# A 31-tap depthwise convolution as three of half length, with the tap tables, the LayerNorm mean and the block order changed beside it

## The chip, the cores and the metric

The kernel runs on one core of a Trainium2 chip. The metric is the device time of one execution in microseconds; the time shown is the median of three runs. A core has five engines with instruction streams of their own: TensorE (PE; its weight loads are listed as PEld), VectorE (DVE), ScalarE (ACT), GpSimd (POOL) and SyncE (SP), which issues all DMAs of this kernel.

## What is computed

One layer of a hybrid encoder block, f32, 1024 positions, width 1024. The part that matters here is the mixer with the long convolution, which runs beside a gated delta rule over 8 heads:

```python
h = rms_norm(x, g_mix); proj = h @ w_in      # columns: glu_a glu_b q k v z a_in b_in gate_a gate_b
c = glu_a * sigmoid(glu_b)
c = depthwise_conv(c, conv_dw_w) + conv_dw_b                 # 31 taps, centred, per channel
c = silu(layer_norm(c, conv_ln_g, conv_ln_b)); y_conv = c @ w_conv_out
q, k, v = split(silu(depthwise_conv(qkv, qkv_conv_w)))       # 5 taps
o = delta_rule(q, k, v) + reverse(delta_rule(reversed))      # then rms_norm * silu(z)
y = sigmoid(gate_a) * y_conv + sigmoid(gate_b) * (o @ w_delta_out)
x = x + y @ w_o                              # then a SwiGLU feed-forward, an embedding, a last RMSNorm
```

## The kernel before, in words

**Layout.** Activations lie transposed: 128 channels on partitions, positions along the free axis. A block column is 128 output channels of one projection: `block_half` makes 24 products of 128x128 by 512 for each half of the positions (8 slices of the contraction, three products each, since an f32 operand is split into a high and a low f32r part, `split`, L693). So a block column is 48 products.

**An order written out by a planner.** The program does not issue instructions directly. Each call (`pn.matmul`, `pn.act`, `pn.stt`, ...) adds an operation with an engine, a cost and a rank (`pn.level`); `Plan.order` (L346) then lays them out as a list scheduler: on each engine the ready operation with the lowest rank goes first, then the earlier one in the program. Each engine's order is fixed by that before the kernel runs; DMAs are issued on SP in planned order too. The ranks are in `LV` (L572): weights -3.0, delta rule -1.8, z 0.5, GLU 1.2, q/k/v 1.3, LayerNorm 2.1, gates 2.3, output projection of the convolution (cout) 2.4, and last the 31-tap convolution, 2.7. Tiles are planned as well: a request waits until its pool has a free buffer and its kind is under its cap (`CAP`, L573). The pool of large tiles (128 x 1024 f32) has `N_BIG` = 32 buffers: 16 hold the normed input as high and low parts, 1 the sum for the LayerNorm (`lnacc`), at most `N_D` = 11 belong to the delta rule; the rest is for block columns in flight.

**The stages.** Start: x is loaded, transposed and normed; tap tables are built (L825 to L838: 24 transposes of 5 taps into `cw5`, 8 of 31 taps into `cw31`). Then the block columns of `MAIN` and `FILL` (L597) in that program order: q, k, v (`do_qkv`, L912: projection, 5 taps on VectorE, SiLU, store), g (`do_glu`, L929), z and the gates a and b; `conv_out` (L1293); and the delta rule, four groups of two heads, whose chain steps are short f32 products with VectorE and ScalarE between them. By rank the delta rule goes first wherever it is ready and block columns fill in. The first block column's weights are loaded ahead (`first_w`, L792), at a fixed place, that of k0.

**The 31 taps.** `do_glu` writes the gated product into a tile padded by 15 positions on each side and calls `conv` (L896): the first tap on ScalarE with the bias, then 30 multiply-adds on VectorE, each over 1024 positions, each onto the one before (`scalar_tensor_tensor`). The result is stored to DRAM and added to `lnacc`.

**The LayerNorm.** `conv_out` waits for all eight blocks: it sums `lnacc` over channels by 8 products with one column of ones (`sums`, L753), scales, spreads the mean over partitions by 8 products with the identity (`rows`, L746), and for each half of the positions reads the blocks back, subtracts, squares and sums, then normalises, applies SiLU and projects by `w_conv_out` (cout: 8 x 24 products per half).

**After it.** The delta output projection (from L1398), with `OT_AFTER` and `WO_AFTER` tying its loads to stores of cout; then `w_o`, with `YT_AFTER` (which store its input's loads wait for) and `WO_LEAD` (how many output blocks start on the first half of the contraction before the second), the feed-forward, the embedding and the output.

L243 and L248 are the helpers of products and transposes, L268 and L275 those of ScalarE, L291 that of VectorE: in the profile all work has these lines, and the tiles tell it apart.

## Time and profile before

| | us |
|---|---|
| median of 3 runs (2107.71 to 2111.0) | 2109.98 |
| the profiled execution | 2112.86 |
| its span, first to last instruction | 2111.1 |
| busy: PE, PEld, DVE, ACT, POOL | 2071.5, 1701.3, 1639.3, 1143.8, 129.1 |

Busy time counts a matmul from its start to its modelled end, so a TensorE that is slowed down between products can look busy. The idle time of an engine that isn't the bottleneck costs nothing. DMA engines move 139 GB/s on the mean.

### The profile page before, as it was taken

The numbers are of one execution on the slowest core, as the hardware profiler recorded it, in microseconds if no ns is written. First come the engines' busy times: TensorE is split into PE (matmuls) and PEld (weight loads), VectorE is DVE, ScalarE is ACT, GpSimd is POOL, SyncE is SP. The second block draws the span as 40 slices with busy tenths as digits, with TensorE's granted clock in tenths as the row PEclk, the third lists the DMA queues.
The fourth block names the chain that finished last, engine by engine and source line by source line (L and its number), as shares of the span: only waits on it lengthen the run. The fifth ranks groups of instructions, "written<-read, shape, count | busy, mean of one in ns | idle before, by whom it ended". The sixth has DMA issues, their size and how long they took to land.

```text
span 2111.1 us, 29502 instructions
## 1 busy us (share of the span) xinstructions
PE 2071.5 (98%) x10279; PEld 1701.3 (81%) x10279; DVE 1639.3 (78%) x2683; ACT 1143.8 (54%) x2603; POOL 129.1 (6%) x197
## 2 busy tenths in 40 slices
PE   8999999999999999999999999999999999999998
PEld 6888888788888788878877788887777777777888
DVE  5578969877999899996687767787666657888776
ACT  6726674657766664857875444433333335443542
POOL 1000111011200211001100000000000000000000
PEclk9999999999999999999999999999999999999999
DMA  6334332533333421544567686433333337442253
GB/s 220 126 102 134 106 118 68 179 95 111 135 101 115 140 83 68 199 149 161 165 206 234 204 278 209 127 120 105 100 96 104 100 99 264 154 160 80 66 161 104
DMA packets 296726, 292.85 MB, mean 139 GB/s; under 512 B 17945, under 2 KB 217810, under 8 KB 296576
## 3 DMA queue, kind: packets, MB, share of 16 engines
q1 hardware_dynamic: 296576, 290.95, 42.8%
q8 instruction: 81, 1.33, 0.3%
q14 instruction: 69, 0.57, 0.1%
HBM read 205.10 MB, written 85.79 MB: 138 GB/s over the span
## 4 chain that ended last, share of the span: by engine, by line
PE 64%; DVE 6%; ACT 4%; issue 1%; DMA 1%; POOL 0%; DVEq 0%; SPq 0%; POOLq 0%; ACTq 0%
PE ps L243 63%; DVE big L291 4%; ACT big L268 2%; PE ps L248 1%; DVE mid L291 1%; DVE w L291 1%; ACT big L275 1%; ACT w L268 0%; ACT m L275 0%; DMA raw<-in_w_delta_out_dram 0%; ACT mid L268 0%; POOL rn L320 0%; DMA mid<-d 0%; DMA big<-dqkv 0%; DMA big<-dg 0%
## 5 line engine op out<-in xcount | busy, mean ns | idle before, releaser
L243 PE MATMUL ps<-big,w 128*128 128x512 f32 (+1 forms) x7416 | 1825.7, 400 | 5.7 <-ACT w L268 3.9
L243 PEld LDWEIGHTS ps<-big,w 128*128 128x128 f32 x7416 | 1360.2, 189 | 316.6 <-ACT w L268 5.8
L291 DVE SCALAR_TENSOR_TENSOR big<-big,cw 128x1024 f32<-128x1024 f32 x336 | 433.5, 1295 | 17.3 <-ACT big L275 11.2
L268 ACT CAST w<-raw 128x512 fp32r<-128x512 f32 (+2 forms) x308 | 185.5, 607 | 275.0 <-PE ps L243 225.8
L291 DVE TENSOR_TENSOR w<-raw,w 128x512 fp32r<-128x512 f32 (+2 forms) x308 | 208.9, 681 | 85.9 <-ACT w L268 83.1
L268 ACT CAST w<-mid 128x512 fp32r<-128x512 f32 (+1 forms) x185 | 108.3, 588 | 153.6 <-PE ps L243 121.9
L291 DVE TENSOR_TENSOR big<-big 128x512 fp32r<-128x512 f32 (+2 forms) x238 | 161.5, 702 | 12.0 <-ACT big L268 8.4
L291 DVE TENSOR_TENSOR w<-mid,w 128x512 fp32r<-128x512 f32 (+1 forms) x185 | 118.7, 644 | 60.3 <-ACT w L268 59.4
L291 DVE TENSOR_TENSOR big<-ps,big 128x512 f32<-128x512 f32 (+1 forms) x146 | 99.9, 687 | 36.6 <-PE ps L243 27.2
L268 ACT CAST big<-big 128x512 fp32r<-128x512 f32 x163 | 96.2, 622 | 43.7 <-DVE big L291 23.3
L268 ACT COPY big<-big 32x128 f32<-32x128 f32 (+1 forms) x264 | 103.1, 441 | 18.7 <-DVE big L291 16.8
L243 PE MATMUL ps<-big 128*128 128x128 f32 (+1 forms) x784 | 104.6, 280 | 7.8 <-ACT big L268 5.1
L243 PEld LDWEIGHTS ps<-big 128*128 128x128 f32 x784 | 98.9, 191 | 16.4 <-issue 11.2
L268 ACT COPY big<-ps 128x512 f32<-128x512 f32 (+3 forms) x178 | 74.9, 429 | 65.3 <-PE ps L243 56.2
L275 ACT ACTIVATE mid<-mid 128x512 f32<-128x512 f32 (+2 forms) x87 | 50.4, 584 | 51.9 <-DVE mid L291 28.4
L243 PEld LDWEIGHTS ps<-S,big 128*128 128x128 f32 x448 | 69.2, 190 | 11.4 <-DVE S L291 2.9
L243 PE MATMUL ps<-S,big 128*128 128x128 f32 x448 | 74.9, 276 | 0.6 <-DVE S L291 0.6
L268 ACT COPY m<-ps 128x512 f32<-128x512 f32 x52 | 30.4, 587 | 76.8 <-PE ps L243 76.7
L268 ACT COPY mid<-ps 128x512 f32<-128x512 f32 x71 | 41.1, 585 | 55.5 <-PE ps L243 45.7
L248 PE MATMUL ps<-ident,big 128*128 128x128 f32 (+2 forms) x368 | 61.1, 280 | 9.9 <-DMA big<-in_x_dram 4.9
L243 PEld LDWEIGHTS ps<-big,m 128*128 128x128 f32 x512 | 62.6, 194 | 7.6 <-ACT m L275 5.3
L275 ACT ACTIVATE big<-big 128x1024 f32<-128x1024 f32 (+2 forms) x80 | 56.7, 718 | 22.0 <-DVE big L291 18.6
(161 smaller groups left out, 1717.6 us busy)
## 6 DMA issues: line engine op xcount, KB each, us to landing
raw<-in_w_in_dram SPq DMA_DIRECT2D x128, 256.0 KB, 3.1
mid<-d SPq DMA_DIRECT2D x120, 256.0 KB, 3.6
d<-big SPq DMA_DIRECT2D x119, 256.0 KB, 3.0
big<-d SPq DMA_DIRECT2D x119, 256.0 KB, 5.1
d<-mid SPq DMA_DIRECT2D x100, 256.0 KB, 2.1
big<-dqkv SPq DMA_DIRECT2D x32, 512.0 KB, 5.1
raw<-in_w_gate_up_dram SPq DMA_DIRECT2D x50, 256.0 KB, 3.1
dqkv<-big SPq DMA_DIRECT2D x24, 512.0 KB, 2.6
```

Source lines behind the costliest of these rows:

```text
L243: o = self.add("pe", lambda: self.nc.tensor.matmul(out.ap(), lhsT.ap(), rhs.ap(), start=start, stop=stop, **kw), [out], [lhsT, rhs], cost)
L248: self.add("pe", lambda: self.nc.tensor.transpose(out.ap(), in_.ap(), ident.ap()), [out], [in_, ident], 0.11)
L268: return self.nc.scalar.copy(out.ap(), in_.ap())
L275: return self.nc.scalar.activation(out.ap(), in_.ap(), func, **kw)
L291: return getattr(e, name)(**{k: v.ap() if isinstance(v, View) else v for k, v in kw.items()})
```

## The change

The 31 taps are split into even and odd positions. With even taps w0, w2, ... (16) and odd taps w1, w3, ... (15), and the padded input kept as its odd places `co` and even places `ce`, three sums of half length give both results: u = (w_even + w_odd) on co; the even outputs are u plus the even taps on ce - co; the odd outputs are u plus the odd taps on (ce one place on) - co. So a block takes 15 + 16 + 15 multiply-adds over 512 elements and two subtractions over 527 and 526, instead of 30 over 1024; the first tap on ScalarE is 512 wide. The last multiply-adds of the two results write at stride two into the tile that held the padded input, which is the block's output from then on (`acc = c[:, :T]`). A tile `dif` holds the two differences.

The 5-tap and 31-tap rows are loaded into one tile and turned by 8 transposes of 46 rows into one table `taps`; sums of neighbouring taps are added up in `cw31s`. The LayerNorm's mean comes from one f32 product of the 128x128 ones with `lnacc` for each half, which gives it on all partitions at once. The first block's weights follow the order's first entry (now q0). Ranks, caps, the order of blocks, `YT_AFTER` and `WO_LEAD` have new values.

```diff
@@ -569,8 +569,8 @@
 
 
 N_BIG, N_MID, N_W, N_D = 32, 8, 6, 11
-LV = dict(w=-3.0, logits=-0.2, delta=-1.8, qkv=1.3, glu=1.2, z=0.5, conv31=2.7, gate=2.3, pl=-0.3, ln=2.1, cout=2.4)
-CAP = dict(raw5=6, acc5=3, cpad=10, acc31=1, lnev=3, wmain=4, wfill=2, bank=2, x0=4)
+LV = dict(w=-3.6, logits=-0.2, delta=-1.8, qkv=1.3, glu=1.5, z=0.5, conv31=3, gate=2.3, pl=-0.3, ln=0.9, cout=2.4)
+CAP = dict(raw5=6, acc5=3, cpad=10, acc31=1, dif=1, lnev=3, wmain=4, wfill=2, bank=2, x0=4)
 LEAD = (1, 3, 3)
 PAIRS = (3, 3, 3)
 NS = sum(PAIRS)
@@ -581,8 +581,8 @@
 WO_AFTER = 12
 RE_CAP = 3
 O_CAP = 4
-YT_AFTER = (2, 1)
-WO_LEAD = 6
+YT_AFTER = (1, 1)
+WO_LEAD = 5
 WO_BANKS = 6
 FIN = 3
 X_LEVEL = -4
@@ -594,9 +594,9 @@
 
 
 
-MAIN = ("k0 q0 v0 l0 g0 z0 k1 q1 z2 v1 g1 z1 q3 k2 g2 v3 v2 q2 k3 k4 q4 z3 z4 a4 k5 g3 v5 z6 v4 g4 "
-        "v6 q5 k7 q6 a5 g5 a7 k6 z5 z7 g6 v7 g7 a6 q7")
-FILL = "a0 a2 a3 a1 b0 b1 b2 b3 p0 b4 b5 b6 b7"
+MAIN = ("q0 k0 v0 l0 g0 z0 k1 q1 z2 v1 g1 g2 z1 k2 v3 v2 q3 z3 q2 k3 k4 a4 z4 q4 k5 g3 v5 z6 v4 g4 v6 q5 "
+        "k7 q6 g6 a5 g5 a7 k6 z5 v7 g7 a6 q7 z7")
+FILL = "a0 a2 b5 b7 a3 a1 b2 b0 b1 b3 p0 b4 b6"
 PL_AFTER = 2
 
 
@@ -686,8 +686,8 @@
     e_t = const("e_t", [P, 16, NJ])
     e_l = const("e_l", [P, 16, NJ])
     pl_r = const("pl_r", [P, NJ])
-    cw31 = const("cw31", [P, KB, CK])
-    cw5 = const("cw5", [P, 24, SK])
+    taps = const("taps", [P, KB, CK + 3 * SK])
+    cw31s = const("cw31s", [P, KB, CK // 2 + 1])
 
 
     def split(hi, lo, src, scale=None):
@@ -789,7 +789,8 @@
 
     n = vectors(0, VEC[:1])
     pn.stream = "main"
-    first_w = [load_w(w_in[0], 0, KB, C_Q + NH * P)]
+    first = MAIN.split()[0]
+    first_w = [load_w(w_in[0], 0, KB, C_Q + ("qkv".index(first[0]) * NH + int(first[1:])) * P)]
     pn.stream = "start"
     for t in range(4, 8):
         pn.dma(x0[t], x[0, t * P:(t + 1) * P, :])
@@ -822,20 +823,20 @@
 
     to(0.9, "tables")
     vectors(n, VEC[1:])
-    ps = bank()
+
+    NT = CK + 3 * SK
+    raw = large([NT, D], line="taps")
+    pn.dma(raw[:CK], conv_dw_w[0])
     for i in range(3):
-        c5 = large([SK, D], line="taps", cap=2)
-        pn.dma(c5, qkv_conv_w[0, :, i * D:(i + 1) * D])
-        for k in range(KB):
-            o = (i * KB + k) * SK
-            pn.transpose(ps[:, o:o + SK], c5[:, cs(k)], ident[:SK, :SK])
-    pn.copy(cw5, ps[:, :24 * SK].fold(24, SK))
-    c31 = large([CK, D], line="taps", cap=2)
-    pn.dma(c31, conv_dw_w[0])
+        pn.dma(raw[CK + i * SK:CK + (i + 1) * SK], qkv_conv_w[0, :, i * D:(i + 1) * D])
     ps = bank()
     for k in range(KB):
-        pn.transpose(ps[:, k * CK:(k + 1) * CK], c31[:, cs(k)], ident[:CK, :CK])
-    pn.copy(cw31, ps[:, :KB * CK].fold(KB, CK))
+        pn.transpose(ps[:, k * NT:(k + 1) * NT], raw[:, cs(k)], ident[:NT, :NT])
+    pn.copy(taps, ps[:, :KB * NT].fold(KB, NT))
+    cw31 = taps[:, :, :CK]
+
+    pn.tt(cw31s[:, :, :CK // 2], taps.at(0, [(NT, KB), (2, CK // 2)]), taps.at(1, [(NT, KB), (2, CK // 2)]), ALU.add)
+    pn.copy(cw31s[:, :, CK // 2:], cw31[:, :, CK - 1:])
 
 
     d_g = dp.tile([P, P], tag="dg", bufs=1)
@@ -920,11 +921,34 @@
         pn.fill(raw[:, 0:2], 0.0)
         pn.fill(raw[:, T + 2:T + 4], 0.0)
         acc = large(line="acc5", cap=CAP["acc5"])
-        conv(acc, raw, cw5[:, b], SK)
+        conv(acc, raw, taps[:, hd, CK + which * SK:CK + (which + 1) * SK], SK)
         pn.act(acc, acc, AF.Silu)
         pn.dma(d_qkv[which][hd], acc)
 
     lnacc = large(line="lnacc")
+    CH = (T + CK - 1) // 2
+
+    def conv31(c, b):
+
+
+
+        w, ws = cw31[:, b], cw31s[:, b]
+        co, ce = c[:, :CH], c[:, CH:2 * CH]
+        dif = large([P, 2, CH], line="dif", cap=CAP["dif"])
+        pn.tt(dif[:, 0], ce, co, ALU.subtract)
+        pn.tt(dif[:, 1, :CH - 1], ce[:, 1:], co[:, :CH - 1], ALU.subtract)
+        acc = large([P, 2, HW], line="acc31", cap=CAP["acc31"])
+        u, v = acc[:, 0], acc[:, 1]
+        pn.act(u, co[:, 0:HW], AF.Identity, scale=ws[:, 0:1], bias=col["cb31"][:, b:b + 1])
+        n = CK // 2
+        for t in range(1, n + 1):
+            pn.stt(u, co[:, t:t + HW], ws[:, t:t + 1], u, ALU.mult, ALU.add)
+        for t in range(n + 1):
+            pn.stt(c.at(0, [(2, HW)]) if t == n else v, dif[:, 0, t:t + HW], w[:, 2 * t:2 * t + 1],
+                   v if t else u, ALU.mult, ALU.add)
+        for t in range(n):
+            pn.stt(c.at(1, [(2, HW)]) if t == n - 1 else u, dif[:, 1, t:t + HW], w[:, 2 * t + 1:2 * t + 2],
+                   u, ALU.mult, ALU.add)
 
     def do_glu(b):
         to(LV["glu"], "main", "glu")
@@ -933,15 +957,18 @@
         for h in range(2):
             pn.act(sg[h], block_half(wb, hA, h, KB), AF.Sigmoid)
         wa = load_cols(C_GLUA + b * P)
+
         c = large([P, T + CK - 1], line="cpad", cap=CAP["cpad"])
         for h in range(2):
             pa = block_half(wa, hA, h, KB)
-            pn.tt(c[:, 15 + h * HW:15 + (h + 1) * HW], pa, sg[h], ALU.mult)
-        pn.fill(c[:, 0:15], 0.0)
-        pn.fill(c[:, T + 15:T + 30], 0.0)
+            pn.tt(c.at(7 + h * HW // 2, [(CH + 1, 2), (1, HW // 2)]), pa.at(0, [(1, 2), (2, HW // 2)]),
+                  sg[h].at(0, [(1, 2), (2, HW // 2)]), ALU.mult)
+        pn.fill(c[:, 0:7], 0.0)
+        pn.fill(c[:, CH - 8:CH + 8], 0.0)
+        pn.fill(c[:, 2 * CH - 7:2 * CH], 0.0)
         to(LV["conv31"], "conv31")
-        acc = large(line="acc31", cap=CAP["acc31"])
-        conv(acc, c, cw31[:, b], CK, bias=col["cb31"][:, b:b + 1])
+        conv31(c, b)
+        acc = c[:, :T]
         for h in range(2):
             pn.dma(d_y[b][h], acc[:, hs(h)])
         if b == 0:
@@ -1292,13 +1319,12 @@
 
     def conv_out():
         to(LV["ln"], "fill", "ln")
-        mean = tin.tile([P, NJ], tag="mean", bufs=1)
-        ps = sums(lnacc, NJ)
-        pn.ts(mean, ps[:, :NJ], 1.0 / D, ALU.mult)
         for h in range(2):
             to(LV["ln"], "fill", "ln")
             mb = mid.tile([P, HW], tag="lnb", line="lnb", bufs=3)
-            pn.act(mb, rows(mean[:, 4 * h:4 * h + 4], 4))
+            ps = bank()
+            pn.matmul(ps, ones, lnacc[:, hs(h)], True, True)
+            pn.act(mb, ps, AF.Copy, scale=1.0 / D)
             acc = mid.tile([P, HW], tag="lnb", line="lnb", bufs=3)
 
             def centred(k):
```

## Rows read from the trace of the kernel before

**Rows 1.** Part 1 of the page (busy time, share of the span, instructions of each engine) and, of part 2, the clock granted to TensorE in 40 slices of the span, in tenths of full speed.

```profile
PE 2071.5 (98%) x10279; PEld 1701.3 (81%) x10279; DVE 1639.3 (78%) x2683; ACT 1143.8 (54%) x2603; POOL 129.1 (6%) x197
...
PEclk9999999999999999999999999999999999999999
```

**Rows 2.** Busy time by stretch of the span: length, then busy us and number of instructions of each engine, the granted clock, the share of the DMA engines, GB/s.

```profile
0.00:50.00 50.00, 43.10 (x214) 32.07 (x215) 26.59 (x47) 34.99 (x66) 5.70 (x19) 0.94 0.67 229
...
150.00:950.00 800.00, 788.39 (x4239) 658.45 (x4238) 704.97 (x1133) 508.22 (x1365) 92.25 (x133) 1.00 0.37 120
950.00:1200.00 250.00, 238.72 (x1257) 198.74 (x1256) 185.71 (x330) 176.15 (x402) 19.69 (x24) 0.97 0.60 190
...
1500.00:1750.00 250.00, 250.00 (x1069) 198.65 (x1068) 150.05 (x227) 89.83 (x153) 0.00 (x0) 1.00 0.34 108
2100.00:2111.00 11.00, 1.58 (x13) 1.10 (x11) 4.27 (x11) 3.06 (x9) 1.08 (x2) 0.78 0.26 95
```

**Rows 3.** The same stretches for TensorE's instructions that read a weight tile w alone (apart from the 256-wide ones at the very end these are all products of 512 columns): length, busy us and number, clock, DMA share, GB/s.

```profile
0.00:50.00 50.00, 16.14 (x52) 0.94 0.67 229
...
150.00:950.00 800.00, 663.37 (x2527) 1.00 0.37 120
950.00:1200.00 250.00, 193.28 (x721) 0.97 0.60 190
...
1500.00:1750.00 250.00, 250.00 (x1069) 1.00 0.34 108
2100.00:2111.00 11.00, 0.00 (x0) 0.78 0.26 95
```

**Rows 4.** TensorE's order of time in the delta stage: start us, us, engine, line, operation, out<-in, shape, number of instructions merged.

```profile
1008.69 3.73 PE L243 MATMUL ps<-big,m 128*128 128x128 f32 x32
1012.17 1.41 PE L243 MATMUL ps<-big,w 128*128 128x512 f32 x5
```

**Rows 5.** What TensorE waited for from 150 to 950 us: us in total, number of waits, longest us.

```profile
PE ps L243 <- ACT big L268: 3.8, 3, 1.7
PE ps L243 <- DVE xin L291: 2.7, 4, 0.9
...
PE ps L248 <- DVE m L291: 1.4, 3, 0.7
```

**Rows 6.** TensorE's groups of instructions by shape over the whole span: out<-in, shape, xcount | busy us, mean ns of one | idle us before them. An f32 product is two instructions, an f32 transpose one.

```profile
L243 PE MATMUL ps<-ones,big 128*128 128x1 f32 x32 | 3.8, 244 | 0.0
...
L248 PE MATMUL ps<-ident,big 5*128 5x5 f32 x24 | 2.3, 203 | 0.0
L243 PE MATMUL ps<-ident,mean 128*128 128x128 f32 x16 | 2.3, 275 | 0.0
...
L248 PE MATMUL ps<-ident,big 31*128 31x31 f32 x8 | 1.0, 225 | 0.1
```

**Rows 7.** VectorE's groups by shape over the whole span: xcount | busy us, mean ns of one | idle us before them.

```profile
L291 DVE SCALAR_TENSOR_TENSOR big<-big,cw 128x1024 f32<-128x1024 f32 x336 | 433.5, 1295 | 17.3 <-ACT big L275 11.2
...
L291 DVE TENSOR_TENSOR big<-big 128x512 f32<-128x512 f32 x68 | 46.2, 687 | 2.9 <-DMA big<-d 1.7 <-DVE w L291 0.4 <-DMA d<-big 0.3
...
L291 DVE SCALAR_TENSOR_TENSOR mid<-ps,vec_t,mid 128x512 f32<-128x512 f32 x16 | 11.3, 745 | 0.4 <-PE ps L248 0.3
...
L291 DVE TENSOR_TENSOR mid<-mid 128x128 f32<-128x128 f32 x2 | 0.6, 292 | 0.1
...
L291 DVE TENSOR_TENSOR mid<-ps,bc 128x128 f32<-128x128 f32 x1 | 0.3, 292 | 3.1 <-ACT beta L275 3.1
```

**Rows 8.** VectorE's order of time where eleven taps of one block run one behind the other: start us, us, number merged.

```profile
129.30 14.31 DVE L291 SCALAR_TENSOR_TENSOR big<-big,cw 128x1024 f32<-128x1024 f32 x11
```

**Rows 9.** All instructions that use the tap tables (tile cw: cw5 and cw31): xcount, min/median/max ns, first and last start us. The eight with vec_t are the first tap of a 31-tap block, the 24 without it that of a 5-tap block.

```profile
L291 DVE SCALAR_TENSOR_TENSOR big<-big,cw x336: 1232/1280/1955, 57.6 to 964.2; 128x1024 f32<-128x1024 f32 x168
L275 ACT ACTIVATE big<-big,cw x24: 1131/1151/1177, 55.9 to 863.7; 128x1024 f32<-128x1024 f32 x24
L275 ACT ACTIVATE big<-big,vec_t,cw x8: 1231/1244/1255, 117.6 to 861.2; 128x1024 f32<-128x1024 f32 x8
L291 DVE COPY cw<-ps x2: 274/345/416, 42.2 to 43.8; 128x120 f32<-128x120 f32 x1, 128x248 f32<-128x248 f32 x1
```

**Rows 10.** Busy time from 860 to 960 us, columns as in group 2.

```profile
860.00:960.00 100.00, 98.19 (x456) 78.10 (x456) 95.33 (x160) 67.95 (x160) 6.77 (x7) 1.00 0.52 168
```

**Rows 11.** The order of time between 964 and 982 us, all engines: start us, us, engine.

```profile
967.52 1.17 PE L243 MATMUL ps<-ones,big 128*128 128x1 f32 x10
...
980.26 0.59 ACT L268 COPY lnb<-ps 128x512 f32<-128x512 f32 x1
```

**Rows 12.** Instructions that use the LayerNorm's rows (tile lnb): xcount, min/median/max ns, first and last start us.

```profile
L291 DVE TENSOR_TENSOR mid<-mid,lnb x48: 677/684/693, 984.8 to 1110.6; 128x512 f32<-128x512 f32 x48
```

**Rows 13.** What TensorE waited for from 930 to 1200 us: us in total, number of waits, longest us.

```profile
PE ps L243 <- ACT w L268: 3.9, 3, 3.0
PE ps L243 <- DVE big L291: 2.4, 1, 2.4
PE ps L243 <- DVE lnb L291: 1.8, 1, 1.8
```

**Rows 14.** Busy time in two short stretches of the hand-over, columns as in group 2.

```profile
1025.00:1035.00 10.00, 8.45 (x45) 7.49 (x46) 4.65 (x8) 9.25 (x18) 0.00 (x0) 0.83 0.51 160
1150.00:1160.00 10.00, 9.04 (x27) 6.90 (x28) 9.85 (x17) 5.38 (x10) 0.00 (x0) 0.66 0.62 195
```

## The prediction

> **What bounds it now.** I read the page's busy shares first [rows 1]: TensorE is busy 98% of the span at nearly its full clock, VectorE 78%, ScalarE 54%. So the end is set by TensorE, and VectorE matters only where TensorE waits for it. A busy TensorE can still hide gaps, so I priced its work by pieces. From 1500 to 1750 us nothing interrupts it: 1069 products of 512 columns in 250 us, 0.234 us each [rows 2, 3]. In the delta stage 32 passes of 128 columns start 3.48 us ahead of the next group, 0.109 us each [rows 4]. With these two prices (everything that reads no weight tile counted as a 128-wide pass) I subtracted the work of each stretch from its length. What is left is room:
> - 0 to 50 us: 50 - 52 x 0.234 - 162 x 0.109 = 20.2 us, start-up;
> - 150 to 950 us (projections beside the delta rule): 800 - 2527 x 0.2339 - 1712 x 0.109 = 22.3 us;
> - 950 to 1200 us (last delta heads, LayerNorm, both output projections): 250 - 721 x 0.234 - 536 x 0.109 = 22.9 us;
> - 1500 to 1750 us: none, by construction; 2100 us to the end: 9.6 us of drain, which the change doesn't touch.
>
> The room is larger than the idle time that the rows show (11.6 us and 11.3 us in the two middle stretches [rows 2]). The Trainium skill says the same of this kind of row (Perfetto Trace Analysis, Identifying the Most-Contended Engine): a matmul's busy share is no good measure of headroom, the share of weight loading is better. By that share alone, 81%, some 400 us would seem to be free; here the trace disagrees, since the uninterrupted stretch has only 79% of it too, 198.7 of 250 us [rows 2].
>
> So an edit pays if it removes TensorE work, or closes part of the 22 and the 23 us.
>
> **TensorE's own work.** The taps: 24 transposes of 5x5 (2.3 us) and 8 of 31x31 (1.0 us) [rows 6] become 8 of 46x46. I bound these by the 31x31 row: 0.125 us of busy time each, or 0.225 us if none overlapped, so 1.0 to 1.8 us. That saves 1.5 to 2.3 us, but in the start-up stretch, which has room of its own; I take 1.5, with ends 0 and 2.3. The LayerNorm mean: half of the 32 row sums against ones (1.9 us) and 16 instructions that spread the mean (2.3 us) [rows 6] go. Two f32 products of 512 columns come, four instructions; the trace has none. Each costs between the 512-wide product, 0.234 us, and four 128-wide f32 passes, 0.44 us. I take the upper end, 1.8 us together, since the type is the same as there. Saved: 2.4 us, ends 1.7 (both old parts at 0.109 per instruction) and 3.3. Together **-4 us**, ends -2 and -6.
>
> **VectorE.** A 31-tap block now issues 30 taps of 1024 elements, 1.29 us each: 38.7 us busy [rows 7]; run one behind the other they are 1.30 us apart [rows 8]. It becomes 15 + 16 + 15 = 46 taps of 512, for which I take the 512-wide form with a scalar column, 0.745 us: 34.3 us. The two differences of 527 elements cost the 512-wide subtraction, 0.687 us, and a little: 1.4 us [rows 7]. So 35.7 us, 3.0 us less per block, 24 us over eight. The two 512-wide results written at stride two, and the gated product that reads PSUM at stride two, are priced as dense ones: the only strided PSUM read, 128 elements from ps, takes 292 ns, as does the dense one in SBUF [rows 7]. Below 24 I keep 18: with the same 10 ns between dependent taps as now (39.0 against 46 x 0.755 + 1.4 = 36.1, or 2.9) and some 0.7 us per block for strides; above it 30, where other work fills the ends of the taps.
>
> How much reaches TensorE between 150 and 950 us? VectorE is busy 705 of 800 us there, so taps do queue in front of other work, but TensorE's direct waits for VectorE are only 4.1 us (xin and m); the 3.8 us behind ScalarE may have VectorE behind them [rows 5]. Shorter taps also hold a delta-chain step up by 0.7 instead of 1.3 us. I take **-4 us**, ends 0 (all hidden behind TensorE) and -11 (half of the room).
>
> ScalarE's first tap falls from 1.24 us for 1024 to half the elements, eight times [rows 9]: some 3 us saved, priced at nothing, as ScalarE is 54% busy. Eight more fills on POOL, 6% busy, nothing either: they come before a block's taps, which wait on VectorE far longer.
>
> **The hand-over.** Here I expect most. The last 31-tap block starts at 861.2 us and ends at 964 [rows 9], because its taps have the lowest rank and VectorE is 95% busy meanwhile [rows 10]. Only then can the LayerNorm begin: the sums against ones start at 967.5, the mean's row is copied out at 980.3 [rows 11], and the subtractions and products with the rows run from 985 to 1111 [rows 12]. The convolution's output projection, the only fill left for the last heads, hangs on them; so TensorE waits 2.4 and 1.8 us behind VectorE at the delta chain's end, 3.9 us for split weights after it [rows 13], and runs part of the time at the lower clock, 1.2 GHz: granted 0.83 and 0.66 in two stretches of 10 us [rows 14].
>
> With 24 us less queued on VectorE I expect the last tap 15 to 25 us earlier. The mean needs two products and two copies instead of sums, a scaling, eight spreads and a copy: 12.8 us between its first and last step become 3 (1.8 for the products, two copies of 0.59 [rows 11]) or a little more. The LayerNorm's rank also rises over that of the projections (2.1 to 0.9): its loads and stores on SP, its squares on ScalarE and its differences on VectorE now go ahead of evacuations and stores of q, k, v and gate blocks, not of weight loads, which rank higher still. Few are left to be held up, the last 5-tap block having begun at 863.7 us [rows 9]. GLU blocks drop behind q, k and v (1.2 to 1.5) while the list brings g2 and g6 forward; either moves the last tap by at most a block column, 48 x 0.234 = 11 us, which the ends below take in. So the second half of the output projection, 192 products or 45 us, is ready some 25 us sooner, in time for the waits of 1025 to 1085 us. I take **-10 us** of the 23, ends 0 and -16. What stays: the wait for split weights at the start of the delta output projection, and with it the clock there. That is late next.
>
> **At nothing.** The new first block (q0 for k0) loads as many bytes at the same place. Tables: the first 5-tap block starts at 55.9 us, the tables are copied at 42.2 and 43.8 [rows 9]; now all four loads must land before any transpose, and 12 us of slack cover it. Weight rank -3.6 instead of -3.0: no other rank lies between. The later ranks and counts (WO_LEAD, YT_AFTER) act after 1190 us, where I see no room; they could cost about 2 us.
>
> **Sum.** The profiled execution took 2112.9 us, 2.9 above the median of the runs. 2112.9 - 4 - 4 - 10 = 2094.9; less 2.9, **2092 us** (-0.9%). All good ends: 2112.9 - 6 - 11 - 16 - 2.9 = 2077.
>
> **Rivals.**
> 1. The hand-over closes as far as it can, and half the middle: 2079 to 2077. For: conv end, mean and rank all pull one way. Against: the weights' wait at 1150 us isn't touched. 14%.
> 2. The relief stays on VectorE. Every engine's order is fixed in advance, and VectorE's 95% in the last 100 us [rows 10] is not taps alone. Only TensorE's 4 us are gained: 2106. 14%, about a third of it beyond -0.2%.
> 3. More instructions, no relief. If a 512-wide tap cost over 0.81 us, 46 of them and the differences would equal 38.7 us, and the LayerNorm would gain only the mean's 9 us; at 0.90 us VectorE would get 33 us more and the hand-over 10 us worse: 2112.9 - 4 + 10 - 2.9 = 2116. The rows speak against it: between 512 and 1024 elements 0.55 us, hence 0.2 us fixed, 18 more instructions 3.6 us, against 6144 elements less, 6.5 us. 4%. The Trainium skill has the rule behind this rival (VectorE: DVE Perf Modes, Rules for kernel authors): for chained operations keep the count of operations low. By it alone 48 instead of 30 would lose; no row shows a chain of taps of that length.
> 4. Buffers run out; this is the slower case. Of 32 large tiles the normed input holds 16, the LayerNorm sum 1, delta up to 11; four are left. A 31-tap block now holds three (padded input, kept as output until stored; differences; accumulator) instead of two. A q, k or v block then waits for its tile while low-ranked taps crawl, 100 us in the last block. A block column is 48 products, 11 us; gates cover it only while they last. The gain of 18 us is gone at 2.2 us lost per block; at 5.5 us it would be 2092 + 44 = 2136, at 3.5 us 2120. Against: the tile caps keep one of each, and eight blocks in 800 us leave gaps. 12%.
>
> **How the numbers follow.** Forecast 2092 with 56%. Under 0.2% (4.2 us) a measurement can hardly tell a change from none. Faster: 56 + 14 + 5 = 75%; same: 9%; slower: 4 + 12 = 16%. The range from 2077 to 2110 takes in rivals 1 and 2 and the bounds; it leaves out rivals 3 and 4.
>
> **What would show it.** 368 taps of 512 at about 0.75 us and VectorE's total near 1615 us; the last tap before 950 us, the last LayerNorm product before 1090; busy TensorE from 950 to 1200 us up by 5 us or more; instructions that spread the mean gone. Wrong: taps above 0.81 us, a last tap as late as 960, or a new TensorE wait for ScalarE's evacuation of q, k or v blocks (rival 4).

## The result, and the profile after

| | us | against before, 95% interval |
|---|---|---|
| median before (4 runs, 2107.71 to 2111.38) | 2110.49 | |
| median after (4 runs, 2083.02 to 2085.64) | 2084.0 | 0.9877 [0.986, 0.9895] |
| the profiled execution after; its span | 2085.64; 2083.9 | |

The change takes 26.5 us off. The forecast was 2092 us, so 8 us of gain were not foreseen. The range holds the time, but a large part of the gain comes from another place than the prediction says, as the experiments show.

The busy time of the engines, from the page of after (answers to [rows 1]):

```profile
PE 2050.6 (98%) x10227; PEld 1692.2 (81%) x10227; DVE 1605.8 (77%) x2827; ACT 1140.2 (55%) x2603; POOL 119.7 (6%) x205
```

TensorE loses 20.9 us and VectorE 33.5 us of busy time. The shares hardly move, and the clock is at nine tenths or more in all 40 slices as before, so this part tells nothing of the reason.

After by stretch of the span: length, busy us and number of instructions of PE, PEld, DVE, ACT and POOL, granted clock, DMA share, GB/s (answers to [rows 2, 14]):

```profile
0.00:50.00 50.00, 40.60 (x181) 29.64 (x182) 26.50 (x47) 32.66 (x62) 4.52 (x20) 0.93 0.67 228
150.00:950.00 800.00, 791.68 (x4318) 663.55 (x4317) 698.45 (x1301) 515.46 (x1406) 89.11 (x150) 1.00 0.37 121
950.00:1200.00 250.00, 245.69 (x1242) 204.14 (x1241) 190.56 (x342) 174.71 (x375) 14.59 (x15) 0.99 0.65 210
1025.00:1035.00 10.00, 10.00 (x65) 8.93 (x65) 7.63 (x17) 9.65 (x29) 2.25 (x2) 1.00 0.42 139
1150.00:1160.00 10.00, 9.33 (x40) 6.96 (x39) 10.00 (x18) 5.75 (x11) 0.00 (x0) 1.00 0.48 149
1500.00:1750.00 250.00, 249.67 (x1077) 199.86 (x1076) 150.70 (x230) 92.92 (x160) 0.00 (x0) 1.00 0.38 123
```

In the hand-over (950 to 1200 us) TensorE is busy 245.7 us where it was 238.7, and both short stretches that ran at 0.83 and 0.66 of the clock are at 1.00. The second of these dips is gone. The first has moved forward and grown smaller, since the delta rule now ends earlier (shown below); it stands in these two stretches of after:

```profile
990.00:1000.00 10.00, 8.70 (x55) 7.43 (x55) 4.66 (x9) 8.74 (x25) 2.75 (x5) 0.96 0.80 271
1000.00:1010.00 10.00, 10.00 (x65) 9.05 (x64) 5.32 (x14) 7.77 (x23) 1.37 (x3) 0.87 0.45 153
```

From 150 to 950 us TensorE gains 3.3 us of busy time and VectorE is nearly as busy as before, 698 for 705 us.

TensorE's instructions that read a weight tile, same stretches (answers to [rows 3]):

```profile
0.00:50.00 50.00, 16.11 (x52) 0.93 0.67 228
150.00:950.00 800.00, 653.66 (x2481) 1.00 0.37 121
950.00:1200.00 250.00, 213.91 (x857) 0.99 0.65 210
1500.00:1750.00 250.00, 249.67 (x1077) 1.00 0.38 123
```

The last line is the one that no part of the prediction has. In the uninterrupted stretch, whose work was not changed, 1077 products run in 249.67 us, 0.2318 us each, where 1069 ran in 250, 0.2339 us.

The taps and the differences on VectorE over the whole span (xcount | busy us, mean ns | idle us before; answers to [rows 7]):

```profile
L291 DVE SCALAR_TENSOR_TENSOR big<-big,taps 128x512 f32<-128x512 f32 x248 | 175.8, 750 | 1.6
L291 DVE SCALAR_TENSOR_TENSOR big<-big,taps 128x1024 f32<-128x1024 f32 x96 | 124.1, 1297 | 12.5 <-ACT big L275 10.1
...
L291 DVE SCALAR_TENSOR_TENSOR big<-big,cw31s 128x512 f32<-128x512 f32 x120 | 93.3, 778 | 3.7 <-ACT big L275 1.8
...
L291 DVE TENSOR_TENSOR big<-big 128x526 f32<-128x526 f32 x8 | 6.0, 756 | 0.0
...
L291 DVE TENSOR_TENSOR big<-big 128x527 f32<-128x527 f32 x8 | 5.6, 703 | 0.7 <-POOL big L324 0.7
```

368 taps of 512 take 175.8 + 93.3 = 269.1 us, 0.73 us on the whole (0.750 and 0.778 by the rows' own means, in which neighbours overlap a little). With the differences a block takes 269.1/8 + 1.5 = 35.1 us of busy time; 35.7 was forecast.

TensorE's groups that took the place of [rows 6], the first of them the mean's products:

```profile
L243 PE MATMUL ps<-big,ones 128*128 128x512 f32 x4 | 2.0, 594 | 0.0
L243 PE MATMUL ps<-ones,big 128*128 128x1 f32 x16 | 2.0, 230 | 0.0
...
L248 PE MATMUL ps<-ident,big 46*128 46x46 f32 x8 | 1.3, 280 | 0.9 <-ACT big L268 0.9
```

When the parts of the hand-over start: first the taps and the table's copy, then the LayerNorm's products with its rows (xcount, min/median/max ns, first and last start us; answers to [rows 9, 12]):

```profile
L291 DVE SCALAR_TENSOR_TENSOR big<-big,taps x344: 710/747/2265, 58.0 to 932.9; 128x512 f32<-128x512 f32 x124, 128x1024 f32<-128x1024 f32 x48
...
L291 DVE COPY taps<-ps x1: 531/531/531, 47.2 to 47.2; 128x368 f32<-128x368 f32 x1
```

```profile
L291 DVE TENSOR_TENSOR mid<-mid,lnb x48: 678/685/694, 942.6 to 1090.8; 128x512 f32<-128x512 f32 x48
```

The last tap starts at 932.9 us instead of 964.2, the LayerNorm begins at 942.6 instead of 984.8 and ends at 1090.8 instead of 1110.6.

The delta chain's state S and the loads of `w_conv_out`, columns as above. First the kernel before:

```profile
L291 DVE SCALAR_TENSOR_TENSOR S<-S,e_l,ps x96: 304/343/350, 255.2 to 1070.1; 128x128 f32<-128x128 f32 x96
```

```profile
L340 SPq DMA_DIRECT2D raw<-in_w_conv_out_dram x32: 368/426/571, 1006.8 to 1141.9; - x32
```

The same two groups after:

```profile
L291 DVE SCALAR_TENSOR_TENSOR S<-S,e_l,ps x96: 333/346/349, 242.6 to 1022.4; 128x128 f32<-128x128 f32 x96
```

```profile
L340 SPq DMA_DIRECT2D raw<-in_w_conv_out_dram x32: 368/416/462, 1039.7 to 1127.0; - x32
```

The delta rule ends 48 us earlier (1022.4 for 1070.1), and cout begins **later**, 1039.7 for 1006.8. So cout does not fill the last heads sooner, as the prediction had it; it hardly fills them at all. What fills them is block columns of the order that were not done yet: from 950 us to the first load of `w_conv_out` TensorE does 190 weight products after and 118 before. The stretch of cout is then nearly without a gap, as three windows of after show (columns as above):

```profile
1000.00:1050.00 50.00, 50.00 (x298) 43.61 (x298) 38.79 (x81) 39.70 (x97) 5.06 (x5) 0.97 0.51 165
1050.00:1100.00 50.00, 50.00 (x225) 40.63 (x225) 39.09 (x64) 40.62 (x62) 1.40 (x1) 1.00 0.83 262
1100.00:1150.00 50.00, 48.00 (x208) 38.38 (x207) 38.40 (x63) 25.57 (x46) 0.00 (x0) 1.00 0.76 246
```

TensorE's waits after, first from 150 to 950 us, then from 930 to 1200 us (us in total, number, longest; answers to [rows 5, 13]):

```profile
PE ps L243 <- ACT big L268: 3.3, 6, 1.5
...
PE ps L248 <- DVE m L291: 0.8, 2, 0.6
```

```profile
PE ps L243 <- ACT w L268: 2.0, 2, 1.2
```

The waits for VectorE's `big` and `lnb` at the delta chain's end are gone; of the wait for split weights 2.0 of 3.9 us are left.

### The profile page after: what moved, and what is told of

Same layout as the page of the kernel before. It is cut to its first block, busy times and chain, and to the rows that moved or that the text cites. A ratio compares the mean times of both kernels' runs of the same rounds, so it can differ in the third digit from the quotient of the medians.

```text
span 2083.9 us, 29572 instructions
## 1 busy us (share of the span) xinstructions
PE 2050.6 (98%) x10227; PEld 1692.2 (81%) x10227; DVE 1605.8 (77%) x2827; ACT 1140.2 (55%) x2603; POOL 119.7 (6%) x205
## 4 chain that ended last, share of the span: by engine, by line
PE 64%; DVE 9%; ACT 6%; DMA 5%; issue 2%; SPq 0%; POOL 0%; DVEq 0%; POOLq 0%; ACTq 0%
PE ps L243 63%; DVE big L291 5%; ACT big L268 3%; DMA big<-d 1%; DVE w L291 1%; DVE mid L291 1%; PE ps L248 1%; DMA mid<-d 1%; ACT w L268 1%; ACT big L275 1%; DMA d<-mid 1%; ACT mid L275 1%; DMA big<-dkk 1%; ACT L275 0%; SPq L340 0%
## 5 line engine op out<-in xcount | busy, mean ns | idle before, releaser
L243 PE MATMUL ps<-big,w 128*128 128x512 f32 (+1 forms) x7416 | 1806.6, 397 | 4.7 <-ACT w L268 2.0
L291 DVE SCALAR_TENSOR_TENSOR big<-big,taps 128x512 f32<-128x512 f32 (+1 forms) x344 | 299.4, 903 | 14.1 <-ACT big L275 10.1
L291 DVE TENSOR_TENSOR big<-big 128x512 fp32r<-128x512 f32 (+3 forms) x254 | 172.2, 702 | 21.3 <-ACT big L268 14.8
L268 ACT COPY big<-ps 128x512 f32<-128x512 f32 (+3 forms) x178 | 74.7, 428 | 45.7 <-PE ps L243 35.7
L291 DVE SCALAR_TENSOR_TENSOR big<-big,cw31s 128x512 f32<-128x512 f32 x120 | 93.3, 778 | 3.7 <-ACT big L275 1.8
L291 DVE TENSOR_TENSOR big<-big,mid 128x512 f32<-128x512 f32 (+11 forms) x158 | 61.9, 392 | 11.2 <-ACT mid L275 6.5
L248 PE MATMUL ps<-ident,big 128*128 128x128 f32 (+1 forms) x344 | 59.5, 288 | 10.1 <-DMA big<-in_x_dram 6.1
```

What stands on the lines that cost most here:

```text
L243: o = self.add("pe", lambda: self.nc.tensor.matmul(out.ap(), lhsT.ap(), rhs.ap(), start=start, stop=stop, **kw), [out], [lhsT, rhs], cost)
L248: self.add("pe", lambda: self.nc.tensor.transpose(out.ap(), in_.ap(), ident.ap()), [out], [in_, ident], 0.11)
L268: return self.nc.scalar.copy(out.ap(), in_.ap())
L291: return getattr(e, name)(**{k: v.ap() if isinstance(v, View) else v for k, v in kw.items()})
```

## The experiments

Two lines were followed: what moved the pace of a product that nobody touched, and which part of the change closed the hand-over. Every run stands against the kernel before on the same chip (medians 2109.2 to 2110.3 us).

### The pace: where the tiles lie

In the built programs the weight tiles begin at byte 203616 of a partition before and at 204096 after: 32 past a multiple of 64, and a multiple of 64. The 32 bytes are the tile `mean` (8 f32), which the change drops. Three kernels move addresses alone and keep the planned order: one more buffer for the small tile `rs` puts 32 bytes ahead of the weight tiles, and a longer constant puts 32 bytes ahead of the large tiles as well.

```diff
# align_before: the kernel before; misalign_after: the kernel after
-            rs = tin.tile([P, 4], tag="rs", bufs=2)
+            rs = tin.tile([P, 4], tag="rs", bufs=3)
# big_shift: the kernel before
-    mark = const("mark", [P, 1])
+    mark = const("mark", [P, 9])[:, 0:1]
```

> The kernel before, with one more 32-byte buffer for rs in the pool of small tiles. Nothing uses it and the planned order stays; only the six weight tiles behind that pool move by 32 bytes, from 32 past a multiple of 64 bytes to a multiple of 64, which is how they lie in the changed kernel (its mean tile, 32 bytes, is gone). Address theory (the 512-wide products are 1% faster in the changed kernel because of where the weights lie, 0.2315 us each against 0.2339 in the uninterrupted stretch): 2096 to 2102 us, the spacing down to 0.231 to 0.232. Rival (the spacing is the execution's or the new order's): 2110 us as before, 0.234.

> The changed kernel with the same 32-byte buffer added, so that its weight tiles lie 32 bytes past a multiple of 64 again. Address theory: the late stages lose the 8.5 us that they had gained and the earlier ones some 2 to 4 us, 2093 to 2098 us, spacing 0.234. Rival: 2084 us, 0.2315.

> The kernel before with the constant tile mark made 32 bytes longer (its rest is not used); the planned order stays. All large and middle tiles, so the moving operands and what ScalarE and VectorE read and write, now start 32 bytes past a multiple of 64, and the weight tiles at a multiple of 64. If only the weights' place sets the products' pace: as align_before, spacing 0.231, about 2102 us. If the moving operand's place does it as well: 0.234 or more, 2110 us or more.

| | weight tiles, large tiles (bytes past a multiple of 64) | median us | ratio to before |
|---|---|---|---|
| before | 32, 0 | 2110 | 1 |
| `align_before` | 0, 0 | 2102.2 | 0.9962 [0.9949, 0.9976] |
| `big_shift` | 0, 32 | 2111.11 | 1.0006 [0.9994, 1.0017] |
| after | 0, 0 | 2084.0 | 0.9877 [0.986, 0.9895] |
| `misalign_after` | 32, 0 | 2089.06 | 0.9899 [0.9885, 0.9914] |

Weight products from 1500 to 1750 us, in that order of kernels without before and after (`align_before`, `misalign_after`, `big_shift`):

```profile
1500.00:1750.00 250.00, 250.00 (x1079) 1.00 0.34 109
```

```profile
1500.00:1750.00 250.00, 250.00 (x1068) 1.00 0.37 119
```

```profile
1500.00:1750.00 250.00, 250.00 (x1069) 1.00 0.34 108
```

1079 with both on a multiple of 64, 1068 and 1069 with either of them off it. So the pace follows the addresses and not the change's arithmetic, and both kinds of tile have to lie well (`big_shift` moves the middle-sized and small tiles with the large ones). It is worth 8 us in the kernel before and about 5 in the kernel after; the intervals of that last pair touch, their paces don't. The text on `misalign_after` expected a loss of 9 to 14 us: 7272 products lose 17 us at this pace, and only some 5 of them show in the time. Which access inside TensorE is slowed down was not tried.

### The taps

`conv_only` is the kernel before with the new convolution alone (its halves of even and odd places and `cw31s`; tables and order are the old ones). `old_conv` is the kernel after with the old one.

```diff
# conv_only
-        acc = large(line="acc31", cap=CAP["acc31"])
-        conv(acc, c, cw31[:, b], CK, bias=col["cb31"][:, b:b + 1])
+        conv31(c, b)
+        acc = c[:, :T]
...
# old_conv: these lines the other way round
```

> The kernel before with the 31 taps as three half-length sums alone; old tap loading, old mean, old ranks and block order, and the weight tiles 32 bytes past a multiple of 64 as before. Theory of the prediction (24 us less on VectorE pulls the LayerNorm forward): about 4 us from the middle and half of the hand-over, 2099 to 2104 us, last tap some 20 us before 964. Rival (the gain at the hand-over is that of ranks and order, the taps were hidden): 2108 to 2112 us.

> The changed kernel with the old 30 taps of 1024 elements and the old padded layout; all else as changed, weight tiles at a multiple of 64 bytes. Theory of the prediction: VectorE gets its 24 us back, the last tap is again near 960 us and the hand-over loses some 8 us: 2090 to 2096 us. Rival (ranks and order did it): 2084 to 2086 us.

`conv_only` took 2106.88 us, 0.9989 [0.9977, 1.0002]; `old_conv` 2107.13 us, 0.9986 [0.9977, 0.9995]. The first lies between its two texts, and its interval holds 1; the second is slower than either of its texts. So the taps are worth some 3 us in the old kernel, which can't be told from nothing, and 23 us in the new one. All engines from 150 to 950 us and from 900 to 950 us, then the taps of `conv_only`, and their first taps on ScalarE:

```profile
150.00:950.00 800.00, 789.17 (x4229) 659.62 (x4228) 679.05 (x1264) 504.20 (x1358) 85.53 (x139) 1.00 0.37 120
900.00:950.00 50.00, 47.62 (x203) 37.38 (x202) 46.13 (x101) 23.38 (x45) 1.42 (x2) 0.97 0.48 153
```

```profile
L291 DVE SCALAR_TENSOR_TENSOR big<-big,cw x344: 708/749/1901, 55.9 to 957.0; 128x512 f32<-128x512 f32 x124, 128x1024 f32<-128x1024 f32 x48
```

```profile
L275 ACT ACTIVATE big<-big,vec_t,cw31s x8: 812/816/842, 115.9 to 856.6; 128x512 f32<-128x512 f32 x8
```

VectorE is relieved by 705.0 - 679.1 = 25.9 us, as priced (24; 28.2 us over the whole span), and yet the last tap comes only 7 us earlier, 957.0, and TensorE is busy as long as before, 789.2 for 788.4 us. The last block starts at 856.6 us (before 861.2 [rows 9]) and still takes 100 us to its last tap, where before it took 103: at the end VectorE remains busy 46 of 50 us with what ranks higher. So most of the relief lies earlier, where TensorE gained nothing by it. In `old_conv` the same relief is missing where the new order needs it (same views, with the start of the hand-over):

```profile
150.00:950.00 800.00, 786.87 (x4276) 660.15 (x4275) 722.54 (x1142) 512.75 (x1385) 99.70 (x141) 1.00 0.36 118
950.00:1000.00 50.00, 43.21 (x257) 37.64 (x257) 27.18 (x59) 32.59 (x106) 5.74 (x7) 0.89 0.25 82
```

```profile
L291 DVE SCALAR_TENSOR_TENSOR big<-big,taps x336: 1240/1282/2272, 54.4 to 951.9; 128x1024 f32<-128x1024 f32 x168
```

VectorE has 24 us more, the last tap starts at 951.9 for 932.9, and in the 50 us after it TensorE is idle for 6.8 us and is granted 0.89 of its clock.

### The order

`ranks_only` is the kernel before with the new `LV`, `MAIN`, `FILL`, `YT_AFTER`, `WO_LEAD` and first block; `old_ranks` is the kernel after with the five old constants.

```diff
# ranks_only, and the first two lines of old_ranks with - and + exchanged
-LV = dict(w=-3.0, logits=-0.2, delta=-1.8, qkv=1.3, glu=1.2, z=0.5, conv31=2.7, gate=2.3, pl=-0.3, ln=2.1, cout=2.4)
+LV = dict(w=-3.6, logits=-0.2, delta=-1.8, qkv=1.3, glu=1.5, z=0.5, conv31=3, gate=2.3, pl=-0.3, ln=0.9, cout=2.4)
...
```

> The kernel before with the new ranks, block order, YT_AFTER and WO_LEAD (and the first block's weights by the order); old taps, old mean, weight tiles 32 bytes past a multiple of 64 as before. Interaction theory (the new order pays only with the shorter taps: each alone moves little, together some 15 us): 2107 to 2116 us. Additive theory (the effects add up: 26 us less 8 for the address, 3 for the taps and 2 to 3 for the mean leave 12 for the order): 2096 to 2101 us.

> The changed kernel with the ranks, block order, YT_AFTER and WO_LEAD of before; new taps, new mean, one tap table, weight tiles at a multiple of 64 bytes. Interaction theory: the kernel before less 8 us (address), 3 (taps alone) and 2 to 3 (mean): 2096 to 2101 us. Theory of the prediction (taps and mean pull the LayerNorm forward whatever the order): 2086 to 2092 us.

`ranks_only` took 2116.72 us, 1.0035 [1.0023, 1.0047], a little above its first text; `old_ranks` 2144.63 us, 1.0168 [1.0155, 1.0181], which neither text held. The new order is a loss of 7 us by itself, and without it the changed kernel is 60 us slower. How much of the 60 is the order's own, `conv_mean` (further down) bears on. `ranks_only` from 1000 to 1050 us:

```profile
1000.00:1050.00 50.00, 43.83 (x275) 39.44 (x276) 27.11 (x61) 45.12 (x122) 7.41 (x9) 0.86 0.45 151
```

Without the relief TensorE still idles 6.2 us there, at a granted clock of 0.86. `old_ranks`, three stretches of 50 us, then TensorE's waits from 930 to 1200 us, the loads of `w_conv_out`, and two neighbouring loads of `w_in` in SP's order of time (start us, us, engine, line, operation):

```profile
900.00:950.00 50.00, 38.45 (x164) 28.98 (x163) 44.51 (x96) 20.47 (x47) 4.29 (x5) 0.93 0.39 121
950.00:1000.00 50.00, 39.41 (x199) 31.81 (x199) 25.33 (x50) 36.86 (x95) 5.65 (x8) 0.84 0.42 137
1000.00:1050.00 50.00, 40.50 (x240) 34.83 (x240) 29.68 (x60) 40.36 (x119) 9.43 (x11) 0.86 0.38 127
```

```profile
PE ps L243 <- DVE big L291: 13.6, 5, 9.1
PE ps L248 <- DVE m L291: 5.9, 1, 5.9
```

```profile
L340 SPq DMA_DIRECT2D raw<-in_w_conv_out_dram x32: 372/411/970, 1092.0 to 1178.3; - x32
```

```profile
964.72 0.42 SPq L340 DMA_DIRECT2D raw<-in_w_in_dram  x1
...
1033.26 0.43 SPq L340 DMA_DIRECT2D raw<-in_w_in_dram  x1
```

TensorE is idle 9.5 to 11.6 us in each 50. The longest wait, 9.1 us of the 13.6 for large tiles that VectorE writes, ends at 946.5 us with the LayerNorm's mean product, which needs the last block's taps (the last one starts at 944.3). After it the fill comes late: SP has no load of `w_in` between the two shown, and from 965 to 1034 us TensorE does 32 weight products, for 138 after. Block columns were not used up, for their last load is at 1084.1 us, and that of cout's weights begins at 1092.0. Why the old order is laid out so badly with the new convolution is not settled; `conv_mean` bears on it.

### The mean, and taps with the mean

`mean_only` is the kernel before with the mean from the 128x128 ones, `no_mean` the kernel after with the old mean (both with the third buffer for `rs`, so that the weight tiles lie as before and as after, measured from a multiple of 64 bytes), `conv_mean` the kernel before with taps and mean.

```diff
# mean_only; no_mean the other way round
-        mean = tin.tile([P, NJ], tag="mean", bufs=1)
-        ps = sums(lnacc, NJ)
-        pn.ts(mean, ps[:, :NJ], 1.0 / D, ALU.mult)
...
-            pn.act(mb, rows(mean[:, 4 * h:4 * h + 4], 4))
+            ps = bank()
+            pn.matmul(ps, ones, lnacc[:, hs(h)], True, True)
+            pn.act(mb, ps, AF.Copy, scale=1.0 / D)
```

> The kernel before with the LayerNorm's mean by two products with ones alone; a 32-byte buffer is added in the place of the mean tile, so that no address of the large, middle and weight tiles moves. Theory of the prediction (the shorter chain lets the LayerNorm begin some 9 us earlier): 2104 to 2107 us. Rival (only TensorE's own work of some 2 us is saved, or less): 2108 to 2110 us.

> The changed kernel with the old mean by sums and rows, padded so that the weight tiles stay at a multiple of 64 bytes. Theory of the prediction: 2 us of TensorE work and some of the 9 us of the chain come back, 2087 to 2091 us. Rival (in the new order the mean's chain is covered by gate columns): 2084 to 2086 us.

> The kernel before with the three half-length sums and the mean by ones, old ranks and order, old loading and turning of the taps, weight tiles 32 bytes past a multiple of 64. It lies between conv_only (2107 us) and old_ranks (2145 us, which has the one tap table and aligned weights as well). If taps and mean together upset the old order (the LayerNorm goes ahead of the gate columns that the last heads need as fill): 2140 to 2152 us. If it is the one tap table: 2102 to 2107 us.

`mean_only` took 2108.49 us, 0.999 [0.9982, 0.9999], 1.4 us less than before: no more than TensorE's own 2 us, although the LayerNorm's products begin 17 us earlier:

```profile
L291 DVE TENSOR_TENSOR mid<-mid,lnb x48: 677/684/1121, 967.8 to 1091.2; 128x512 f32<-128x512 f32 x48
```

`no_mean` took 2092.96 us, 0.9915 [0.9903, 0.9928], 9 us more than after and more than either text held. Its LayerNorm is hardly later than after's (943.4 to 1094.5 us). The loss that the rows show best, 4 us, is where the delta output projection begins, from 1100 to 1150 us, with a longer wait for split weights (TensorE's waits from 930 to 1200 us below):

```profile
1100.00:1150.00 50.00, 43.92 (x178) 34.74 (x178) 37.07 (x59) 26.25 (x46) 0.00 (x0) 0.95 0.73 234
```

```profile
PE ps L243 <- ACT w L268: 5.9, 2, 3.0
```

After is busy 48.00 of these 50 us with the full clock and waits 2.0 us for them. `conv_mean` took 2115.38 us, 1.0029 [1.0018, 1.0041], between the two expectations. Two stretches of it:

```profile
950.00:1000.00 50.00, 45.53 (x271) 38.76 (x270) 29.49 (x57) 39.84 (x108) 8.58 (x12) 0.97 0.56 180
1000.00:1050.00 50.00, 43.86 (x252) 38.08 (x251) 32.44 (x61) 42.58 (x114) 7.28 (x9) 0.90 0.40 134
```

It idles 4.5 and 6.1 us there, about half of what `old_ranks` idles (10.6 and 9.5), though it has the same ranks, taps and mean, and k0 as its first block too. What still differs is the common tap table and the place of the weight tiles, and by the place `old_ranks` should be the faster. So some 30 us of `old_ranks`' loss come with the tap table, through what the planner makes of it, and say nothing of taps or ranks as such. Against `conv_mean` the changed kernel is 31 us faster, with the table and the place of the weight tiles in it, so the order's own share is to be sought there and not at 60. What the table does in the new order was not tried.

### The late ranks and the LayerNorm's rank

```diff
# old_late: the kernel after
-YT_AFTER = (1, 1)
-WO_LEAD = 5
+YT_AFTER = (2, 1)
+WO_LEAD = 6
# ln_rank: the kernel after, in LV
-ln=0.9
+ln=2.1
```

> The changed kernel with YT_AFTER and WO_LEAD of before. By the prediction these are worth nothing, at most 2 us: 2082 to 2086 us. Rival (part of the gain behind the hand-over is theirs): 2087 to 2092 us.

> The changed kernel with the LayerNorm's rank at 2.1 as before. By the prediction the rank pulls the LayerNorm ahead of evacuations and stores: without it 2086 to 2092 us, the last LayerNorm product later than 1091 us. Rival (by then few block columns are left to be passed): 2083 to 2086 us.

`old_late` took 2082.18 us, 0.9865 [0.9848, 0.9881], `ln_rank` 2081.01 us, 0.9867 [0.985, 0.9885]. The first is as the prediction had it, the second below both its texts. Neither can be told from after, so neither edit is shown to have a share in the gain. With the old rank (`ln_rank`) the LayerNorm is where it was with the new one:

```profile
L291 DVE TENSOR_TENSOR mid<-mid,lnb x48: 680/685/694, 940.3 to 1088.2; 128x512 f32<-128x512 f32 x48
```

`ln_rank` has the lowest median of all, but its interval overlaps after's; no version is shown to beat the changed kernel.

### The books by room

The prediction's measure, length less products at their pace less short passes at 0.109 us, for every kernel; the pace is each kernel's own from 1500 to 1700 us (0.2315 us where the tiles lie well, 0.234 us elsewhere). Short passes are all PE instructions that read no weight tile. Room is what is left over, so over all stretches the books close by themselves: they say where the time went, not why. Each row is one profiled execution; the last two, kernels that can't be told from after, show how far rows scatter.

| | products, short passes 150 to 950 | room us | products, short passes 950 to 1200 | room us |
|---|---|---|---|---|
| before | 2527, 1712 | 22.3 | 721, 536 | 22.9 |
| `align_before` | 2531, 1712 | 27.5 | 737, 536 | 21.0 |
| `big_shift` | 2526, 1712 | 23.2 | 721, 536 | 23.1 |
| `conv_only` | 2517, 1712 | 25.3 | 738, 536 | 19.1 |
| `mean_only` | 2528, 1712 | 20.7 | 742, 508 | 20.7 |
| `conv_mean` | 2529, 1712 | 21.8 | 714, 508 | 27.6 |
| `ranks_only` | 2468, 1788 | 27.1 | 774, 460 | 18.6 |
| `old_ranks` | 2455, 1715 | 44.8 | 645, 506 | 45.5 |
| `old_conv` | 2488, 1788 | 29.2 | 746, 432 | 30.2 |
| `no_mean` | 2474, 1872 | 22.6 | 838, 377 | 14.7 |
| `misalign_after` | 2467, 1844 | 21.9 | 860, 378 | 7.6 |
| after | 2481, 1837 | 25.5 | 857, 385 | 9.7 |
| `old_late` | 2470, 1840 | 27.7 | 861, 380 | 9.3 |
| `ln_rank` | 2474, 1844 | 26.3 | 866, 376 | 8.6 |

Three things stand in it. First, the new order has more of the delta rule (the short passes) done by 950 us and keeps products back: 1788 for 1712, and 1837 with the new taps and mean. Second, the hand-over closes from 22.9 us to under 10 only where order, taps and mean come together. Third, a faster pace is lost again where TensorE waits for others: `align_before` has 5 us more room in the middle than the kernel before.

Against before the sum is: 7272 products x (0.2339 - 0.2315) = -17 us of pace; 52 short passes fewer at 0.109 us, -6; hand-over -13; and as room that grew, +3 in the middle, +4 at the start (23.9 for 20.2 us) and +2 behind 1200 us. Together -27, as the two spans have it (2111.1 and 2083.9). The start's part belongs to the execution as much as to the kernel: in `align_before`, granted the full clock in its first 50 us, that room is 17.5 us, for 20.2 us at 0.94 in the kernel before. For `old_conv` against after the two columns give 3.7 + 20.5 = 24 us, measured 23.

## Why the prediction was right or wrong

**TensorE's own work, -4: half right.** The mean's part, -2.4, is not contradicted (`mean_only` 1.4 us, interval 0.2 to 3.8); its four instructions took 2.0 us, 1.8 was put down. The taps' transposes gave nothing: by 150 us the kernel before has done 446 products and the kernel after 445, so the saving went into the start's room, the end that the text put at 0.

**VectorE's price: right.** 24 us were forecast, with bounds of 18 and 30; `conv_only` has 25.9 from 150 to 950 us and 28.2 over the span. Rival 3 is out: 0.75 to 0.78 us for a tap, not 0.81. The Trainium skill's rule for chained operations (VectorE: DVE Perf Modes, Rules for kernel authors: keep the count of operations low) would have had this lose; 48 operations for 30 took less time here, since each works on half the elements (0.75 us for 1.29).

**Between 150 and 950 us, -4: not seen as a gain.** The room there went from 22.3 to 25.5 us, to 21.9 us at the old pace (`misalign_after`). The relief is real in the new order (`old_conv` 29.2 us for 25.5) but pays for what that order costs there (`ranks_only` 27.1 us). In `conv_only` it closes nothing, which is rival 2's mechanism: relief that stays on VectorE.

**The hand-over, -10: right in size, wrong in mechanism.** It closed by 13 us. The step that fell is "With 24 us less queued on VectorE I expect the last tap 15 to 25 us earlier": the relief alone gives 7 us (`conv_only`). The step after it fell too, that the second half of the output projection is then ready for the waits of 1025 to 1085 us: cout now starts at 1039.7 us, after the delta rule. Behind both lies a premise that the rows don't bear out, that cout is the only fill left for the last heads: 118 products of other block columns run after 950 us in the kernel before, and 190 after. What happened is that block columns kept back by the order fill the last heads, the delta rule and the LayerNorm run beside them and finish early, and cout follows in one piece. The room table and the starts show this; that the kept-back products are why the heads end 48 us earlier is an inference from `ranks_only` and `old_conv`, which change the order or the taps as a whole.

**The mean's chain and the LayerNorm's rank.** The chain shrank (last tap to first difference 20.6 us before, 9.7 after), but a LayerNorm that begins 17 us earlier is worth nothing by itself (`mean_only`). The rank brings nothing that `ln_rank` could show.

**What stays at 1150 us: partly wrong.** The clock there is full and the wait for split weights half; `no_mean` has the wait back and a clock of 0.95 from 1100 to 1150 us. So the mean's edit shows there and not at the LayerNorm's start; by which steps of the plan, no run shows.

**At nothing: right** for the late ranks (`old_late`), wrong by omission for the tiles. The prediction treats a tile that is dropped as free; without it the weight tiles lie on a multiple of 64 bytes, and that is the missing term, about 5 us in this kernel (8 in the old one). It is most of the distance from 2092 to 2084. That the forecast came within 8 us is in part luck: the transposes and the middle brought none of the 5.5 us put down for them, and a pace that the text did not know made up for it.

**Rival 4** (buffers run out) did not happen in after, where TensorE waits 3.3 us for ScalarE's `big` for 3.8 before. `old_ranks` is slower still than its slow side (2120 to 2136 us), but its longest wait is that of the mean product for the last taps, and its loads of `w_in` come late; whether buffers hold these up was not tried.

## What to carry to other kernels

Where a planner fixes the order, an edit has no price of its own: the same taps were worth 3 and 23 us, the same order cost 7 us alone and gained several times that with the taps and the mean, so a change of work and its order are to be priced, and measured, together. Before a gain is put down to arithmetic, compare a stretch that the edit doesn't touch; if its pace moved, look at where the tiles lie. Relief on an engine that doesn't set the end counts only from the wait that it ends, not from its busy time.

## What had not been expected of the hardware

A 512-column product of f32r parts takes 0.2315 us when the weight tiles and the large tiles begin on a multiple of 64 bytes, and 0.234 us when either kind lies 32 bytes off (the middle-sized tiles moved with the large ones) (1077 and 1079 products against 1068 and 1069 in 250 us). The placement also moves when nothing near the product was edited: an 8-word tile was enough. And the granted clock fell behind gaps in the hand-over: in the 10 us from 1025 and from 1150 us it was 0.83 and 0.66 before, a mix of the levels 1.2 and 2.4 GHz. Ahead of the second dip, from 1140 us, TensorE was busy 7.99 of 10 us; in the dip it was busy 9.04 us and did 27 instructions. After, it was busy 8.83 us from 1140 us, the clock stayed at 1.00, and in the next 10 us it did 40 instructions in 9.33 us. So a closed gap can give back more than its own length.
